# One more of eight weight pairs multiplied in seven block products, with half of its weight sums added by DMA

## The chip, the cores and the metric

The kernel runs on one core of one Trainium2 chip. The metric is the device time of one execution in microseconds (us), as the median of several runs: 1747.23 us before the change (three runs, 1747.02 to 1747.3).

## The reference

One decoder block on 256 tokens with a model width of 2048, all in float32. Cut to what matters here:

```python
u = rmsnorm(h, norm1_g[l])
proj = u @ w_in[l]                       # 2048 x 16896
...                                      # gated recurrence ya, dilated attention yb
mix = sigmoid(gate_a) * ya + sigmoid(gate_b) * yb
h = h + mix @ w_out[l]
v = rmsnorm(h, norm2_g[l])
h = h + conv_ffn(v, w_up[l], conv_w[l], conv_b[l], w_down[l])

def conv_ffn(u, w_up, conv_w, conv_b, w_down):
    hup = u @ w_up                       # 2048 x 11264
    hc = causal_conv(hup, conv_w, width=3) + conv_b
    a, b = hc[..., :5632], hc[..., 5632:]
    return (gelu(a) * b) @ w_down        # 5632 x 2048
```

## The kernel before, in words

**Weights as one stream.** The host lays all weights out in units of 16 tiles of 128x128 (1 MB, `UNIT`), in the order in which they are used. `load(u)` fetches a unit from HBM into one of three buffers `raw` on SP's DMA queue. `split(u)` makes two float32r parts of it: ACT copies with rounding (`hi`), DVE subtracts (`lo = raw - hi`). Every product is then three matmuls: small part of the activations with `hi`, large part with `hi`, large part with `lo`. `begin_unit(u)` splits units up to two ahead of the one in use (`LOOKAHEAD`) and loads a third. The order in which the engines get their instructions is set by the tile framework's scheduler, and each engine works through its own queue in that order; a buffer is reused only after its last reader.

**The up-projection.** `w_up` is computed in 11 blocks of 512 columns of the first half and the 512 matching columns of the second half. In a block there are eight units, one for each pair of 128-row slices of `w_up`; a unit holds a 2x2 matrix of blocks of 128x512, named 11, 21, 12, 22. `UP_PAIRS` says how each pair is multiplied:

- mode P: the eight plain block products, 8 x 3 = 24 matmuls (`PRODUCTS["P"]`). Its unit is split into two halves of 1024 columns.
- mode S: seven block products in the manner of Strassen, 7 x 3 = 21 matmuls (`PRODUCTS["S"]`). They need sums of weight blocks, q1 to q4, which DVE makes in `split_s` out of the loaded unit: four additions of 128x512 (L287, L289, L290, L292), then the splits `sa` (blocks 11 and 21), `se` (22 and q3), `sf` (q2 and q4), each 128x1024, and `sg` (q1), 128x512.

Both modes add into the same seven PSUM banks, `sums[1..7]`. The matching sums of the activations are made once, by `operands`, while the product with `w_out` runs, and kept for all blocks (`hv`). `sevenfold` runs the eight units of a block. `unfold` (L535 to L546) turns the seven sums into the four blocks of the result on ACT and DVE. `hidden_side` then transposes, convolves, gates and splits the result, spread over the following units. From block 2 on, two groups of `w_down` products (`dn`, four units) stand between one block and the next; they write into PSUM banks that `unfold` has read out. Between blocks 0 and 1 and between 1 and 2 no `dn` products stand.

Split halves live in rings of buffers: `hi` and `lo` with four buffers each (`wp`), and for mode S also `se` with four and `sg` and `q` with one.

Of the kernel before, what the change touches and what calls it, by code (L numbers as in the profile page):

```python
# [42 lines left out]
SIDE_US = 1.8  # L43
ALIGN = 136
WARM = 12
# [4 lines left out]
def up_order(b):  # L50

    return (1, 3, 0, 4, 2, 6, 5, 7) if b == 0 else tuple(range(KD // 2))

# [116 lines left out]
def hybrid_block(ctx, tc, x_p, x_t, weights, g1, gf, params, c_rope, c_mask0, c_mask1, c_level, out):  # L170
# [15 lines left out]
    def w4(shape, name, dt=F32):  # L186
        return sb.tile([P] + list(shape), dt, tag="w4", name=name, bufs=21)

    def stage(name):
        return late["stage"].tile([P, 512], F32, tag="o2", name=name, bufs=STAGES)  # L190

    def w1(name, n=T, dt=F32):
        return sbe.tile([P, n], dt, tag="w1", name=name, bufs=10)

# [28 lines left out]

    raws, splits, late = {}, {}, {}
    last = [None, None]
# [16 lines left out]
    def load(u):  # L242
        if u >= NUNITS or u in raws:
            return
        r = wp.tile([P, UNIT * P], F32, tag="raw", name=f"raw{u}", bufs=3)
        n = (4, 2)[u] if u < 2 else 1
        w = UNIT * P // n
        for q in range(n):
            nc.sync.dma_start(r[:, q * w : (q + 1) * w], weights[u, :, q * w : (q + 1) * w])
# [19 lines left out]
    def two_parts(hi, lo, src):  # L269

        act.activation(hi, src, AF.Copy)
        vec.tensor_tensor(lo, src, hi.bitcast(F32), op=ALU.subtract)

    def split_s(u):

        r = raws[u].rearrange("p (b n) -> p b n", b=4)
        pool = late["pool"]

        def pair_tiles(pl, tags, name):
            return [pl.tile([P, 2, 512], F32R, tag=t, name=f"{name}{n}{u}", bufs=b) for n, (t, b) in zip("hl", tags)]  # L280

        q1 = pool.tile([P, 512], F32, tag="q", name=f"q{u}", bufs=1)
        ah, al = pair_tiles(wp, (("hi", 4), ("lo", 4)), "sa")
        eh, el = pair_tiles(pool, (("se", 4), ("se", 4)), "se")
        fh, fl = pair_tiles(pool, (("se", 4), ("se", 4)), "sf")
# [4 lines left out]
        vec.tensor_tensor(r[:, 0], q1, r[:, 2], op=ALU.add)  # L290
# [4 lines left out]
        splits[u] = {  # L295
            "11": (ah[:, 0], al[:, 0]), "21": (ah[:, 1], al[:, 1]), "22": (eh[:, 0], el[:, 0]),
            "q3": (eh[:, 1], el[:, 1]), "q2": (fh[:, 0], fl[:, 0]), "q4": (fh[:, 1], fl[:, 1]), "q1": (g[:, 0], g[:, 1]),
        }

    def split(u):  # L300
# [8 lines left out]
        for s in range(2):  # L309
            hi = wp.tile([P, half], F32R, tag="hi", name=f"hi{u}_{s}", bufs=4)  # L310
            lo = wp.tile([P, half], F32R, tag="lo", name=f"lo{u}_{s}", bufs=4)
            n = 2 if u == 0 else 1
# [163 lines left out]
    def moving(parts, k0, nk, name, pst=None):  # L476
# [218 lines left out]
    def hgrn_side(g, f, k, q, gt, v):  # L695
# [22 lines left out]
        for li, b in enumerate(LEVELS):  # L718
            ps = side_bank(f"lv{g}_{b}")
            psv = ps.rearrange("p (m h t) -> p m h t", m=2, h=HG)  # L720
            ks = sbe.tile([P, M], F32, tag="o2", name=f"ks{g}_{b}", bufs=6)
            act.activation(
# [36 lines left out]
        for m in range(2):  # L759
            po = side_bank(f"ho{g}_{m}")  # L760
            for h in range(HG):
# [3 lines left out]
                pe.matmul(dst, ad[:, m, h], v[:, m, cols], start=(m == 0), stop=True)  # L765
            sq = sbe.tile([P, M], F32, tag="o2", name=f"osq{g}_{m}", bufs=6)
            act.activation(sq, po, AF.Square)
# [5 lines left out]
            vec.reciprocal(sd, sd)  # L773
            o1 = sbe.tile([P, HG, P], F32, tag="o2", name=f"oo{g}_{m}", bufs=6)
            vec.tensor_tensor(
# [159 lines left out]
    def late_bank(i, name):  # L935
        return bank(place[i], name)
# [47 lines left out]
    for b in range(NBLK):  # L984
# [4 lines left out]
        for j, b0, b1 in DOWN.get(b, ()):  # L989
            if b1 == NBLK and not gfb:  # L990
                drain()
                for i in range(2):
                    gfb.append(w4([2, 512], f"gfb{i}"))
                    nc.gpsimd.dma_start(gfb[i].rearrange("p a n -> p (a n)"), gf[:, i * 1024 : (i + 1) * 1024].to_broadcast([P, 1024]))
            pst = moving(ff_parts, b0 * FB, (b1 - b0) * FB, f"dn{b}_{j}", [late_bank(i, f"dn{b}_{j}_{i}") for i in ((4, 3) if j % 2 else (1, 5))])
            for m in range(2):
# [61 lines left out]
```

## Time and profile before

| | before |
|---|---|
| median of 3 runs | 1747.23 us |
| the profiled execution: time, and its span | 1748.37 us, 1746.6 us |
| busy: TensorE (PE) | 1730.5 us, 99% of the span |
| busy: VectorE (DVE) | 1287.3 us, 74% |
| busy: ScalarE (ACT) | 943.0 us, 54% |
| mean granted TensorE clock | 0.996 |
| DMA, mean | 188 GB/s |

The profile is of one execution. Busy times are shares of its span; the remaining 1.8 us of that execution lie outside the span. The up-projection and the `dn` products fill the span from about 1047 us on. In the profile, a matmul of 512 columns is shown with a duration of 0.39 us, but matmuls are pipelined: what one costs is the distance from its start to the next one's start. Queues of an engine's DMA issues are named with a q (SPq).

### The profile page before, as it was taken

Reading aid. Unit: us, or ns where it says so; the run is one execution under the profiler, and the core shown is the slowest. Engines: PE = TensorE matmul, PEld = TensorE weight load, DVE = VectorE, ACT = ScalarE, POOL = GpSimd, SP = SyncE. Lnnn points to the kernel's source line nnn. Section 1 sums busy time; section 2 is a strip of 40 time slices with the busy share of each in tenths; the row PEclk is TensorE's granted clock in tenths of the full one; section 3 lists DMA queues with packets and bytes.
Section 4 is the critical chain, followed back from the end, with each engine's and each line's share of the span. In section 5 each row is a group of like instructions: output and inputs, shape, how many; then the busy total and the mean of one; then the engine's idle time right before and its main releaser. Section 6 shows DMA issues by size and latency. Waiting matters only on the chain.

```text
span 1746.6 us, 21480 instructions
## 1 busy us (share of the span) xinstructions
PE 1730.5 (99%) x8373; PEld 1446.3 (83%) x8373; DVE 1287.3 (74%) x1612; ACT 943.0 (54%) x1166; POOL 9.6 (1%) x25
## 2 busy tenths in 40 slices
PE   9999999999999999999999999999999999999997
PEld 8888888888888888888888888788888888888885
DVE  7765575776858675444656699998988988988975
ACT  6444465555455555444444566665655655655653
POOL 0000000000000000000000000000000000000000
PEclk9999999999999999999999999999999999999998
DMA  7665634444444444556455555445545545546652
GB/s 277 231 204 202 231 141 149 169 169 170 168 169 169 169 168 169 191 194 241 176 188 190 179 207 193 166 175 213 197 165 217 198 164 217 199 162 217 226 183 97
DMA packets 48374, 328.05 MB, mean 188 GB/s; under 512 B 5600, under 2 KB 5856, under 8 KB 10128
## 3 DMA queue, kind: packets, MB, share of 16 engines
q1 hardware_dynamic: 45648, 318.28, 50.7%
q0 software_dynamic: 1472, 5.24, 1.0%
q10 hardware_dynamic: 1152, 3.15, 0.5%
q8 instruction: 66, 1.08, 0.2%
q14 instruction: 36, 0.29, 0.0%
HBM read 321.41 MB, written 2.10 MB: 185 GB/s over the span
## 4 chain that ended last, share of the span: by engine, by line
PE 97%; DVE 2%; DMA 0%; ACT 0%; SPq 0%; issue 0%; DVEq 0%
PE up L527 9%; PE up L525 9%; PE up L526 9%; PE dn L472 5%; PE dn L473 5%; PE dn L474 5%; PE egp L474 3%; PE egp L473 3%; PE egp L472 3%; PE ak L385 3%; PE aq L385 2%; PE wo L474 2%; PE gp L472 2%; PE wo L473 2%; PE gp L473 2%; PE gp L474 2%
## 5 line engine op out<-in xcount | busy, mean ns | idle before, releaser
L319 DVE TENSOR_TENSOR lo<-raw,hi 128x1024 fp32r<-128x1024 f32 (+1 forms) x536 | 651.2, 1218 | 371.7 <-ACT hi L318 363.4
L318 ACT ACTIVATE hi<-raw 128x1024 fp32r<-128x1024 f32 (+1 forms) x536 | 565.7, 1056 | 651.9 <-PE up L526 102.4
L474 PE MATMUL dn<-lo,ff 128*128 128x512 f32 x352 | 138.6, 394 | 0.0
L472 PE MATMUL dn<-hi,ff 128*128 128x512 f32 x352 | 138.3, 395 | 0.0
L473 PE MATMUL dn<-hi,ff 128*128 128x512 f32 x352 | 137.6, 391 | 0.0
L527 PE MATMUL up<-lo,hva 128*128 128x512 f32 x330 | 129.6, 393 | 0.0
L525 PE MATMUL up<-hi,hva 128*128 128x512 f32 x330 | 129.4, 392 | 0.0
L526 PE MATMUL up<-hi,hva 128*128 128x512 f32 x330 | 129.3, 392 | 0.0
L472 PE MATMUL egp<-hi,xu 128*128 128x512 f32 x256 | 100.5, 393 | 0.0
L474 PE MATMUL egp<-lo,xu 128*128 128x512 f32 x256 | 99.8, 390 | 0.0
L473 PE MATMUL egp<-hi,xu 128*128 128x512 f32 x256 | 99.7, 389 | 0.0
L472 PEld LDWEIGHTS dn<-hi,ff 128*128 128x128 f32 x352 | 66.1, 188 | 16.1 <-DVE up5c L544 0.4
L474 PEld LDWEIGHTS dn<-lo,ff 128*128 128x128 f32 x352 | 66.1, 188 | 13.5
L473 PEld LDWEIGHTS dn<-hi,ff 128*128 128x128 f32 x352 | 66.2, 188 | 13.1
L525 PEld LDWEIGHTS up<-hi,hva 128*128 128x128 f32 x330 | 62.1, 188 | 12.6
L527 PEld LDWEIGHTS up<-lo,hva 128*128 128x128 f32 x330 | 62.1, 188 | 12.6
L526 PEld LDWEIGHTS up<-hi,hva 128*128 128x128 f32 x330 | 62.0, 188 | 12.7
L385 PE MATMUL ak<-xu,hi 128*128 128x512 f32 x192 | 68.0, 399 | 0.0
L474 PEld LDWEIGHTS egp<-lo,xu 128*128 128x128 f32 x256 | 48.1, 188 | 9.9
L473 PEld LDWEIGHTS egp<-hi,xu 128*128 128x128 f32 x256 | 48.1, 188 | 9.7
L472 PEld LDWEIGHTS egp<-hi,xu 128*128 128x128 f32 x256 | 48.1, 188 | 9.7
L386 PE MATMUL ak<-xu,lo 128*128 128x256 f32 x192 | 54.0, 281 | 0.0
(548 smaller groups left out, 3876.5 us busy)
## 6 DMA issues: line engine op xcount, KB each, us to landing
raw<-weights SPq DMA_DIRECT2D x298, 1024.0 KB, 4.8
h<-x_t ACTq DMA_DIRECT2D x4, 512.0 KB, 5.9
xt<-x_p SPq DMA_DIRECT2D x3, 512.0 KB, 10.0
xs_q<-aqraw POOLq DMA_DIRECT2D x6, 256.0 KB, 6.8
xs_k<-akraw POOLq DMA_DIRECT2D x6, 256.0 KB, 7.0
raw<-weights SPq DMA_DIRECT2D x4, 256.0 KB, 4.8
raw<-weights SPq DMA_DIRECT2D x2, 512.0 KB, 6.9
gfb<-gf POOLq DMA_DIRECT2D x2, 512.0 KB, 5.3
```

The source lines that it names most:

```text
L318: last[0] = act.activation(hi[:, q * w : (q + 1) * w], raw, AF.Copy)
L319: last[1] = vec.tensor_tensor(lo[:, q * w : (q + 1) * w], raw, hi[:, q * w : (q + 1) * w].bitcast(F32), op=ALU.subtract)
L385: pe.matmul(ps, hi, pair, start=(k == 0), stop=False, skip_group_check=True)
L386: pe.matmul(ps[:, T:], lo, pair[:, :T], start=False, stop=(k == nk - 1), skip_group_check=True)
L472: pe.matmul(pst[m], xl, hi, start=(k == k0), stop=False)
L473: pe.matmul(pst[m], xh, hi, start=False, stop=False)
L474: pe.matmul(pst[m], xh, lo, start=False, stop=(k == k0 + nk - 1))
L525: pe.matmul(sums[b], xl, wh, start=b in fresh, stop=False)
L526: pe.matmul(sums[b], xh, wh, start=False, stop=False)
L527: pe.matmul(sums[b], xh, wl, start=False, stop=left[b] == 0)
```

## The change

- `UP_PAIRS`: four pairs of eight are in mode S instead of three, alternating S and P. `up_order` takes the pairs of a block as P, S, P, S, P, S, P, S (block 0: P, P, S, P, S, P, S, S), where before a block began with S and ended with P.
- `load` of an S unit: block b[3] goes into its place in `raw` and a second time into a buffer `q`; the other three blocks follow in one DMA. Two DMAs issued by GpSimd (POOL) then add on arrival: b[2] onto b[3] (this is q3), b[0] onto `q` (this is q1). DVE keeps two of the four additions (q2 and q4).
- `split` and `split_s` take all buffers out of one ring, `pair`, of [128, 2, 1024] (hi and lo in one): four buffers up to the start of the up-projection and six from then on. `q` gets two buffers.
- The seven products of mode S stand in another order, and the `dn` products with odd j write into the banks of sums 6 and 7 instead of 4 and 3.
- Room: `ALIGN` 136 to 8, `w4` 21 to 22 buffers, `w1` 10 to 8, `o2` 6 to 5 in the recurrence, and `stage` 8 to 6 buffers before the up-projection.

```diff
-UP_PAIRS = "SPSPPSPP"
+UP_PAIRS = "SPSPSPSP"
...
-    return (1, 3, 0, 4, 2, 6, 5, 7) if b == 0 else tuple(range(KD // 2))
+    return (1, 3, 0, 5, 2, 7, 4, 6) if b == 0 else (1, 0, 3, 2, 5, 4, 7, 6)
...
+        if MODES.get(u) == "S":
+            b = [weights[u, :, i * 512 : (i + 1) * 512] for i in range(4)]
+            q1s[u] = late["hv"].tile([P, 512], F32, tag="q", name=f"q{u}", bufs=2)
+            nc.sync.dma_start(r[:, 3 * 512 :], b[3])
+            nc.sync.dma_start(q1s[u], b[3])
+            nc.sync.dma_start(r[:, : 3 * 512], weights[u, :, : 3 * 512])
+            nc.gpsimd.dma_start(r[:, 3 * 512 :], b[2], accum_op=ALU.add)
+            nc.gpsimd.dma_start(q1s[u], b[0], accum_op=ALU.add)
+            raws[u] = r
+            return
...
+    def pair_tile(name):
+        more = late.get("pool")
+        n = ring[0] % (6 if more else 4)
+        ring[0] = (n + 1) if more else (n + 1) % 4
+        pool, bufs = (wp, 4) if n < 4 else (more, 2)
+        return pool.tile([P, 2, 1024], F32R, tag="pair", name=name, bufs=bufs)
...
-        vec.tensor_tensor(q1, r[:, 0], r[:, 3], op=ALU.add)
-        two_parts(ah, al, r[:, 0:2])
-        vec.tensor_tensor(r[:, 3], r[:, 3], r[:, 2], op=ALU.add)
-        vec.tensor_tensor(r[:, 0], q1, r[:, 2], op=ALU.add)
-        two_parts(eh, el, r[:, 2:4])
-        vec.tensor_tensor(r[:, 1], r[:, 1], r[:, 0], op=ALU.add)
-        two_parts(fh, fl, r[:, 0:2])
+        b11, b21 = parts(f"sa{u}", r[:, 0:2])
+        b22, q3 = parts(f"se{u}", r[:, 2:4])
+        vec.tensor_tensor(r[:, 0], q1, r[:, 2], op=ALU.add)
+        vec.tensor_tensor(r[:, 1], r[:, 1], r[:, 0], op=ALU.add)
+        q2, q4 = parts(f"sf{u}", r[:, 0:2])
         g = pool.tile([P, 2, 512], F32R, tag="sg", name=f"sg{u}", bufs=1)
         two_parts(g[:, 0], g[:, 1], q1)
...
-        "S": ((1, "a11", "11"), (7, "x3", "q3"), (6, "x2", "q2"), (2, "a12", "21"), (4, "a22", "q4"), (5, "x1", "q1"), (3, "x4", "22")),
+        "S": ((1, "a11", "11"), (2, "a12", "21"), (7, "x3", "q3"), (3, "x4", "22"), (6, "x2", "q2"), (4, "a22", "q4"), (5, "x1", "q1")),
...
-            pst = moving(..., [late_bank(i, ...) for i in ((4, 3) if j % 2 else (1, 5))])
+            pst = moving(..., [late_bank(i, ...) for i in ((6, 7) if j % 2 else (1, 5))])
```

How the loads of a block now stand in the queues. On SP before, in block 5, one DMA for each unit (`raw` numbers are the buffers' running numbers; 10210, 10318 and 10468 are units in mode S, the others P):

```order
L249 DMA raw_10210<-weights 128x2048
L249 DMA raw_10273<-weights 128x2048
L249 DMA raw_10318<-weights 128x2048
L249 DMA raw_10385<-weights 128x2048
L249 DMA raw_10427<-weights 128x2048
L249 DMA raw_10468<-weights 128x2048
```

On SP now, in block 7 (S units: `raw` 10906, 11015, 11107, 11181, with their `q` numbered one higher):

```order
L253 DMA raw_10906<-weights 128x512
L255 DMA raw_10906<-weights 128x1536
L261 DMA raw_10962<-weights 128x2048
L253 DMA raw_11015<-weights 128x512
L255 DMA raw_11015<-weights 128x1536
L254 DMA q_11108<-weights 128x512
L261 DMA raw_11071<-weights 128x2048
L253 DMA raw_11107<-weights 128x512
L255 DMA raw_11107<-weights 128x1536
L254 DMA q_11182<-weights 128x512
L261 DMA raw_11152<-weights 128x2048
```

And on POOL now, the adding DMAs of the same units; before, POOL had nothing to do in this part of the program:

```order
L257 DMA q_10907<-weights 128x512
L257 DMA q_11016<-weights 128x512
L256 DMA raw_10906<-weights 128x512
L256 DMA raw_11015<-weights 128x512
L257 DMA q_11108<-weights 128x512
L256 DMA raw_11107<-weights 128x512
L257 DMA q_11182<-weights 128x512
L256 DMA raw_11181<-weights 128x512
```

An S unit now takes three DMAs on SP and two on POOL instead of one on SP; the `q` ones go ahead of their unit, since `q` has a buffer free earlier.

On PE, the end of a block's up-projection and the start of `dn`. Before (block 2), the last product of a block is one of mode P, into sum 3, and the last one into sum 5 stands two products earlier:

```order
L527 MATMUL up_5_8763<-lo_1_9006,hva_8022 128x512
L525 MATMUL up_3_8761<-hi_1_9005,hvd_8023 128x512
L526 MATMUL up_3_8761<-hi_1_9005,hvd_8023 128x512
L527 MATMUL up_3_8761<-lo_1_9006,hvd_8023 128x512
L525 MATMUL up_3_8761<-hi_1_9005,hvd_8023 128x512
L526 MATMUL up_3_8761<-hi_1_9005,hvd_8023 128x512
L527 MATMUL up_3_8761<-lo_1_9006,hvd_8023 128x512
L472 MATMUL dn_0_1_9124<-hi_0_9039,ff_0_8635 128x512
```

Now (block 6), the last product is one of mode S, into sum 5:

```order
L539 MATMUL up_4_10495<-sf_10710,hvs_7673 128x512
L540 MATMUL up_4_10495<-sf_10710,hvs_7673 128x512
L541 MATMUL up_4_10495<-sf_10710,hvs_7673 128x512
L539 MATMUL up_5_10496<-sg_10713,hvx_7674 128x512
L540 MATMUL up_5_10496<-sg_10713,hvx_7674 128x512
L541 MATMUL up_5_10496<-sg_10713,hvx_7674 128x512
L486 MATMUL dn_0_1_10817<-hl_0_10739,ff_0_10054 128x512
```

The `dn` products follow at once; the first 24 of them write into bank 1, and only then comes the one (`dn_0_5`) that reuses the bank of sum 5.

On PE, the boundary between blocks 1 and 2, where no `dn` stands. Before, the next block opens with products of mode S into sums 1, 7, 6 and 1 (11 matmuls, the last five of them here), and then needs the bank of sum 2:

```order
L525 MATMUL up_6_8764<-sfh_8667,hvx_7475 128x512
L526 MATMUL up_6_8764<-sfh_8667,hvx_7475 128x512
L527 MATMUL up_6_8764<-sfl_8668,hvx_7475 128x512
L525 MATMUL up_1_8759<-sah_8767,hvs_7652 128x512
L526 MATMUL up_1_8759<-sah_8767,hvs_7652 128x512
L525 MATMUL up_2_8760<-sah_8663,hvs_7474 128x512
L526 MATMUL up_2_8760<-sah_8663,hvs_7474 128x512
```

Now it opens with two matmuls into sum 1 and goes on with sum 2; the first into sum 5 is the thirteenth matmul (the two into sum 1 ahead of these rows counted, the transpose L963 not):

```order
L539 MATMUL up_2_8417<-hl_0_8325,hva_7174 128x512
L540 MATMUL up_2_8417<-hl_0_8325,hva_7174 128x512
L541 MATMUL up_2_8417<-hl_0_8325,hva_7174 128x512
L539 MATMUL up_2_8417<-hl_0_8325,hva_7174 128x512
L540 MATMUL up_2_8417<-hl_0_8325,hva_7174 128x512
L541 MATMUL up_2_8417<-hl_0_8325,hva_7174 128x512
L963 MATMUL ua1t_8478<-ident,up1c_8403 128x128
L541 MATMUL up_1_8416<-sa_8362,hvs_7158 128x512
L539 MATMUL up_2_8417<-sa_8362,hvs_7158 128x512
L540 MATMUL up_2_8417<-sa_8362,hvs_7158 128x512
L541 MATMUL up_2_8417<-sa_8362,hvs_7158 128x512
L539 MATMUL up_5_8420<-hl_1_8328,hva_7174 128x512
```

The banks of sums 2 and 5 are both written again sooner than before: that of sum 2 after two matmuls instead of 11, that of sum 5 after 12 instead of 17.

More of the change, by code (lines that the diff above doesn't have):

```diff
@@ L186, in w4 @@
     def w4(shape, name, dt=F32):
-        return sb.tile([P] + list(shape), dt, tag="w4", name=name, bufs=21)
+        return sb.tile([P] + list(shape), dt, tag="w4", name=name, bufs=22)
     def stage(name):
-        return late["stage"].tile([P, 512], F32, tag="o2", name=name, bufs=STAGES)
+        return late["stage"].tile([P, 512], F32, tag="o2", name=name, bufs=STAGES if "pool" in late else STAGES - 2)
     def w1(name, n=T, dt=F32):
-        return sbe.tile([P, n], dt, tag="w1", name=name, bufs=10)
+        return sbe.tile([P, n], dt, tag="w1", name=name, bufs=8)
     def small(shape, name, tag, bufs=2):
@@ L222, in pc @@
         return par[:, POFF[name][0] + i : POFF[name][0] + i + 1]
-    raws, splits, late = {}, {}, {}
+    raws, splits, late, q1s = {}, {}, {}, {}
+    ring = [0]
     last = [None, None]
@@ L290, in split_s, with parts @@
-        vec.tensor_tensor(r[:, 0], q1, r[:, 2], op=ALU.add)
-        two_parts(eh, el, r[:, 2:4])
-        vec.tensor_tensor(r[:, 1], r[:, 1], r[:, 0], op=ALU.add)
-        two_parts(fh, fl, r[:, 0:2])
+        pool, q1 = late["pool"], q1s[u]
+        def parts(name, src):
+            t = pair_tile(name)
+            hi, lo = t[:, 0].rearrange("p (b n) -> p b n", b=2), t[:, 1].rearrange("p (b n) -> p b n", b=2)
+            two_parts(hi, lo, src)
+            return [(hi[:, i], lo[:, i]) for i in range(2)]
@@ L309, in split @@
         for s in range(2):
[L310 to L311 removed]
+            t = pair_tile(f"hl{u}_{s}")
+            hi, lo = t[:, 0], t[:, 1]
             n = 2 if u == 0 else 1
```

22 lines of the change are left out of this document (6 added, 16 removed).

## The prediction

> **What bounds the kernel now.** I read the page first, then the waits and the windows of five whole blocks of the up-projection, then single rows. From the page: the span, the busy times, DVE's busy tenths in 40 slices of the span, and the shares by engine of the chain that ended last.
>
> ```profile
> span 1746.6 us, 21480 instructions
> PE 1730.5 (99%) x8373; PEld 1446.3 (83%) x8373; DVE 1287.3 (74%) x1612; ACT 943.0 (54%) x1166; POOL 9.6 (1%) x25
> ...
> DVE  7765575776858675444656699998988988988975
> ...
> PE 97%; DVE 2%; DMA 0%; ACT 0%; SPq 0%; issue 0%; DVEq 0%
> ```
>
> The windows' header, one block and the sum of the five:
>
> ```profile
> core 0: us, PE busy (x) PEld busy (x) DVE busy (x) ACT busy (x) POOL busy (x), PEclk, DMA share, GB/s
> 1275.64:1341.04 65.40, 65.40 (x296) 53.80 (x295) 56.43 (x73) 38.23 (x46) 0.00 (x0) 1.00 0.55 194
> sum 327.04, PE 327.04 PEld 268.96 DVE 282.16 ACT 190.89 POOL 0.00; mean PE 65.41 PEld 53.79 DVE 56.43 ACT 38.18 POOL 0.00
> ```
>
> PE is the chain, 97% of it, and in a block of 65.40 us it is never idle (65.40 busy). DVE has 9 us free in a block, ACT 27 us, the DMA engines about half of theirs. Who waits in those five blocks (engine and line, for whom, us in total, times, longest):
>
> ```profile
> ACT hi L318 <- PE up L526: 53.7, 43, 2.5
> ACT hi L318 <- DMA raw<-weights: 3.5, 5, 0.9
> SPq L249 <- DVE lo L319: 192.9, 45, 7.1
> ```
>
> The splitting waits for PE to free a buffer, seldom for a load; the loads wait for the splitting to free a `raw` buffer. So the feeders run ahead of PE until the rings are full, and what PE no longer has to do is saved as long as this stays so. What one matmul costs is the distance of starts; the timeline has them, and the load of the S unit whose first product (`sah`) is the fourth row of PE:
>
> ```profile
> 1289.11 0.33 SPq L249 DMA_DIRECT2D raw<-weights  x1
> ...
> 1308.24 0.39 PE L525 MATMUL up<-hi,hvd 128*128 128x512 f32 x1
> 1308.47 0.39 PE L526 MATMUL up<-hi,hvd 128*128 128x512 f32 x1
> 1308.69 0.39 PE L527 MATMUL up<-lo,hvd 128*128 128x512 f32 x1
> 1308.92 0.39 PE L525 MATMUL up<-sah,hvs 128*128 128x512 f32 x1
> 1309.15 0.39 PE L526 MATMUL up<-sah,hvs 128*128 128x512 f32 x1
> ```
>
> Four steps take 0.91 us, 0.2275 us each. Counted in program order, the load issued at 1289.11 is this S unit's: 19.8 us ahead of its use.
>
> **The fourth pair in mode S.** A block had 3 x 21 + 5 x 24 = 183 matmuls and gets 4 x 21 + 4 x 24 = 180. Three fewer in each of 11 blocks are 33 x 0.2275 = 7.5 us, all on the path: a block shrinks from 65.40 to 64.72 us. This is the whole gain; the other parts can only eat it.
>
> **DVE and ACT.** Rows of one block (busy us, mean ns):
>
> ```profile
> L319 DVE TENSOR_TENSOR lo<-raw,hi 128x1024 fp32r<-128x1024 f32 x18 | 22.0, 1220 | 8.5 <-ACT hi L318 8.5
> L272 DVE TENSOR_TENSOR sel<-raw,seh 128x1024 fp32r<-128x1024 f32 x3 | 3.7, 1217 | 0.0
> L272 DVE TENSOR_TENSOR sg<-q,sg 128x512 fp32r<-128x512 f32 x3 | 2.0, 683 | 0.0
> L290 DVE TENSOR_TENSOR raw<-q,raw 128x512 f32<-128x512 f32 x3 | 2.0, 681 | 0.0
> L318 ACT ACTIVATE hi<-raw 128x1024 fp32r<-128x1024 f32 x19 | 20.2, 1061 | 22.6 <-PE up L526 11.0 <-PE dn L473 6.9 <-issue 2.5
> L271 ACT ACTIVATE seh<-raw 128x1024 fp32r<-128x1024 f32 x3 | 3.2, 1052 | 0.0
> L271 ACT ACTIVATE sg<-q 128x512 fp32r<-128x512 f32 x3 | 1.9, 622 | 0.0
> ```
>
> DVE: an S unit's subtractions are 3 x 1.217 + 0.683 = 4.33 us, a P unit's 2 x 1.220 = 2.44, so +1.89; additions fall from 12 to 8, -4 x 0.681 = -2.72. DVE goes from 56.43 to 55.6 us of a block of 64.7, 86% as before. ACT: 3 x 1.052 + 0.622 - 2 x 1.061 = +1.66, to 39.9 us, 62%. Neither is on the path, so neither the relief nor the load changes the sum; the cover is the 9 and 25 us that they have free.
>
> **The loads.** An S unit brings 256 (block 3) + 256 (its copy) + 768 + 2 x 256 (the adds) = 1792 KB instead of 1024. Rows for landing (KB each, median us from issue to landing; the last two rows are windows, one of the block's dense part, one from the start of the program):
>
> ```profile
> raw<-weights SPq DMA_DIRECT2D x298, 1024.0 KB, 4.8
> xs_k<-akraw POOLq DMA_DIRECT2D x6, 256.0 KB, 7.0
> gfb<-gf POOLq DMA_DIRECT2D x2, 512.0 KB, 5.3
> lev<-c_level POOLq DMA_DIRECT2D x1, 448.0 KB, 9.2
> 1298.00:1340.00 42.00, 42.00 (x189) 34.73 (x189) 35.16 (x45) 24.37 (x30) 0.00 (x0) 1.00 0.58 210
> 10.00:30.00 20.00, 19.48 (x98) 15.94 (x97) 16.83 (x19) 16.10 (x22) 0.00 (x0) 1.00 0.90 365
> ```
>
> *Bandwidth.* A block has 12 units of 1024 KB; at 0.55 of 65.4 us one costs 3.0 us of all 16 engines. Now they are 12 + 4 x 0.75 = 15, 45 us of 64.7 (0.70). Where S and P alternate, 2.75 units are 8.2 us in the 45 x 0.2275 = 10.2 us that PE takes for a pair of units (0.81); if an add costs twice its bytes, since it also reads its target, 3.25 units are 9.8 us (0.95). The start of the program ran at 0.90. So the load is dense but fits, at the upper end only just.
>
> *Latency.* No row shows an adding DMA. From below it is a POOL DMA of the same stage (`gfb`, 5.3 us); from above the slowest one (`lev`, 9.2) or twice the common 7.0, if the bytes move twice: 14. I take 7.0, the row with the same size. Block 3 lands in 4.8 (the full unit's time), the add 7.0 later, `se` is split in 1.05 + 1.22: 14.1 us after the issue. PE needs it with the third product, 19.8 + 6 x 0.2275 = 21.2 us after the issue. That leaves 7 us.
>
> *Throughput of the three `raw` buffers.* A P unit holds one for at least 4.8 + 2 x 1.06 + 1.22 = 8.1 us, an S unit for 4.8 + 7.0 + 2 x (1.05 + 1.22) + 2 x 0.68 = 17.7. In three pairs of units (30.7 us of PE) each buffer serves one P and one S, 25.8 us. Margin 4.9 us: an add may take up to 11.9 us before the ring, and not PE, sets the pace. By the row I chose it costs nothing.
>
> *Queues.* SP issues 20 DMAs a block instead of 12, at 0.33 us each 2.6 us more, on a queue that mostly waits. A `q` load stands ahead of the next P load and waits for DVE's `sg`; that split comes with the unit whose `raw` buffer the P load waits for anyway, so it delays little. On POOL each add waits for its plain load, and the adds behind it wait too; the plain loads were issued on SP in a compatible order, so no add waits for a load issued after its own. POOL is otherwise idle here.
>
> A rule speaks against the adds. The `gfb` row above is a POOL DMA in this stage, with DVE 87% busy (52.26 of 60 us):
>
> ```profile
> 1590.00:1650.00 60.00, 60.00 (x273) 49.31 (x273) 52.26 (x69) 34.20 (x42) 1.09 (x2) 1.00 0.58 210
> ```
>
> It landed in 5.3 us, so a busy DVE did not hold it. The Trainium skill ("SBUF — State Buffer", section "SBUF: two separate sides") warns that a DMA issued from POOL waits for its descriptors while DVE runs an operation that uses both ports; by that rule each add would land later, and the late-add rival below would be nearer. It names single-source fp32 copies, which the rows above do not contain, so I give it no part of the sum.
>
> **The order of units and products; the rings.** With `dn` between blocks, 24 matmuls (5.5 us) cover the later end of sum 5, and PE does not wait. Between blocks 0 and 1 and between 1 and 2 there is no such cover. The timeline shows the price of that before, and the windows the clock after it:
>
> ```profile
> 1101.39 0.50 PE L525 MATMUL up<-sah,hvs 128*128 128x512 f32 x1 [2.12 <-DVE up1c L542]
> 1098.00:1101.30 3.30, 1.28 (x6) 0.74 (x4) 3.30 (x5) 0.20 (x1) 0.00 (x0) 1.00 0.78 308
> 1101.30:1106.00 4.70, 4.61 (x14) 3.62 (x15) 4.70 (x8) 1.70 (x2) 0.00 (x0) 0.64 0.66 232
> ```
>
> PE waited 2.1 us for `unfold`, and then ran 4.7 us at a clock of 0.64, another 0.36 x 4.7 = 1.7 us: 3.8 us in all. `unfold` was late because DVE was: it has the side work of the last block to do and no `dn` time to do it in, and was busy without a break:
>
> ```profile
> 1090.00:1098.00 8.00, 8.00 (x37) 6.59 (x37) 8.00 (x12) 6.40 (x9) 0.00 (x0) 1.00 0.12 49
> ```
>
> After the change DVE has 0.8 us less to do in such a block and PE 0.7 us less, so DVE is as late as before. From below this is -3.8 (the wait goes). From above, the next block now needs the bank of sum 2 after two matmuls instead of 11 and that of sum 5 after 12 instead of 17, and DVE, which works in order, has the `se` of an S unit ahead of `unfold`. That unit's load goes out when the third unit before it is split; from then on DVE has some 9.4 us of splitting until this `se` (3 x 0.68 + 6 x 1.22), the add lands after 11.8, so DVE stands still for 2.4 us. With a clock drop of 1.7 that is 4.1 us at each of two boundaries, +8.2. I take 0, the row itself: the wait stays. The Trainium skill ("TensorE: Matmul & The Clock Gate", section "Part 1: The HAM clock gate") puts the idle time that halves the clock at about 3.4 us; here 2.1 us of idleness was followed by a low clock, so the measurement decides, and a new wait of 2 us costs nearly double.
>
> The larger `pair` ring takes nothing from PE. Fewer buffers (`w1`, `o2`, `stage`) touch the part before 1047 us, the first 24 slices, where DVE is busy 4 to 8 tenths and PE's order hardly changes: 0, within 1 us either way. The fourth S operand costs some subtractions of 128 columns on DVE, once: 0 under the product with `w_out`.
>
> **Sum.** -7.5. On the profiled execution, 1748.37 - 7.5 = 1740.9; it stood 1.1 us above the median, so the median comes to 1739.7 us.
>
> **Rivals.**
> 1. *The wait at the block boundary vanishes.* For it: `unfold`'s reading of sum 2 now stands right behind that of sum 6 on DVE, ahead of a split. Against: DVE as busy as before. 1739.7 - 3.8 = 1735.9.
> 2. *The boundaries between blocks 0 and 2 eat the gain.* For it: DVE without a break there, the adds ahead of `unfold`, two S units in a row at the end of block 0. Against: before, only one of the two boundaries waited. 1739.7 + 8.2 = 1747.9 at most, half of it 1743.8.
> 3. *The adds land late (slower).* If an add takes 14 us, a buffer's P and S last 32.8 us instead of 25.8, the pace of a pair is 10.9 instead of 10.2 us, and 44 pairs lose 0.7 each: +31, 1770. It decides from 11.9 us for an add on; a pace of 0.17 us more for a pair (7.5 / 44) already eats the gain, which is 12.4 us. For it: nothing shows an add, and the DMA engines are at 0.81 to 0.95. Against: all POOL rows land in 9.2 us or less, and the units of `dn` let the ring catch up.
> That the change does less than it says can be left out: the 33 matmuls are gone from PE's queue.
>
> **Chances.** Forecast 0.50, rival 1 0.15, rival 2 0.17, rival 3 0.18. A difference of 0.2% (3.5 us) is about what a measurement can tell here, so faster (below 1743.7) is 0.65, same 0.17, slower 0.18. The range reaches from 1735.0 (rival 1) to 1750.0, past rival 2 and a ring that is a little too slow; rival 3 at its price lies outside. The forecast alone has 1738 to 1743.
>
> **What would show it.** Right: 33 matmuls fewer; windows of a block at 64.7 us with PE never idle; DVE near 55.6, ACT near 39.9, DMA share near 0.70; POOL adds landing in 6 to 9 us. Wrong: `se` on ACT waiting for DMA in every block, PE waiting for `se` or `sf`, a PE clock below 1.00 inside the blocks, or PE waiting for `unfold` longer than 2 us between blocks 0 and 2.

## The result: 4.2% slower

| kernel | median, us | against before |
|---|---|---|
| before | 1747.26 (4 runs, 1747.02 to 1747.81) | |
| after | 1821.28 (4 runs, 1819.32 to 1824.3) | 1.0418, 95% interval 1.0405 to 1.0431 |

The profiled execution of after took 1824.3 us, its span is 1822.5. The page of after, with span, busy times, the clock in 40 slices, the shares of the chain that ended last, and the two groups of `se` (busy, mean ns, idle time ahead and what ended it):

```profile
span 1822.5 us, 21674 instructions
PE 1749.0 (96%) x8340; PEld 1451.6 (80%) x8340; DVE 1286.4 (71%) x1592; ACT 954.7 (52%) x1188; POOL 86.4 (5%) x113
...
PEclk9999999999999999999999988999999999999998
...
PE 78%; DMA 10%; DVE 7%; ACT 3%; issue 2%; SPq 0%; ACTq 0%; POOLq 0%; DVEq 0%
...
L284 DVE TENSOR_TENSOR se<-raw,se 128x1024 fp32r<-128x1024 f32 x44 | 53.6, 1217 | 61.0 <-ACT se L283 60.8
L283 ACT ACTIVATE se<-raw 128x1024 fp32r<-128x1024 f32 x44 | 46.6, 1058 | 83.7 <-DMA raw<-weights 71.3
```

The 33 matmuls are gone (8373 to 8340), and PE is no longer the whole chain: DMA has 10% of it. `se` on ACT waited 71.3 us for DMA, which is the q3 add. Of seven whole blocks, taken from the first `dn` product of one to that of the next, one window and the sum:

```profile
1308.28:1381.40 73.12, 66.70 (x292) 54.14 (x293) 56.44 (x71) 39.12 (x48) 6.98 (x8) 0.97 0.73 218
sum 505.74, PE 469.83 PEld 381.75 DVE 395.15 ACT 273.81 POOL 49.15; mean PE 67.12 PEld 54.54 DVE 56.45 ACT 39.12 POOL 7.02
```

A block takes 505.74 / 7 = 72.2 us and not 65.4. The timeline shows where in a block; the rows are those of the end of block 5 (columns: start, duration, engine, line, in brackets the idle time ahead and what ended it):

```profile
1351.07 0.33 SPq L253 DMA_DIRECT2D raw<-weights  x1
1357.10 0.33 SPq L261 DMA_DIRECT2D raw<-weights  x1
1357.63 0.88 POOL L256 DMA_DIRECT2D raw<-weights  x1 [6.61 <-DVE sf L284]
1359.37 0.33 SPq L261 DMA_DIRECT2D raw<-weights  x1
1359.92 0.87 POOL L257 DMA_DIRECT2D q<-weights  x1 [1.42 <-DMA q<-weights]
1368.23 1.06 ACT L283 ACTIVATE se<-raw 128x1024 fp32r<-128x1024 f32 x1 [7.45 <-DMA raw<-weights]
1373.61 0.33 SPq L261 DMA_DIRECT2D raw<-weights  x1
1375.13 0.39 PE L541 MATMUL up<-sg,hvx 128*128 128x512 f32 x1
1379.71 1.06 ACT L332 ACTIVATE hl<-raw 128x1024 fp32r<-128x1024 f32 x1 [2.60 <-DMA raw<-weights]
1380.68 0.67 ACT L552 ACTIVATE up5c<-up,rstd_r 128x512 f32<-128x512 f32 x1
1381.40 0.79 PE L486 MATMUL dn<-hl,ff 128*128 128x512 f32 x1 [5.88 <-ACT up5c L552]
1381.99 0.63 PE L487 MATMUL dn<-hl,ff 128*128 128x512 f32 x1
1382.42 0.63 PE L488 MATMUL dn<-hl,ff 128*128 128x512 f32 x1
```

This is the last S unit of the block. Its block 3 is issued at 1351.07 and its q3 add at 1357.63. Loads of 1 MB for `dn` units go out on both sides of the add, at 1357.10 and at 1359.37, and at 1359.92, 2.3 us after it, the `q` add of the next block's first S unit. ACT gets q3 at 1368.23, after 7.45 us of waiting with everything behind it, so a `raw` buffer comes free late (the unit's last split, `sf`, ends on DVE at 1373.58), the next load on SP goes out only at 1373.61, and ACT waits another 2.60 us for that one. Behind that split stands `unfold`'s last read of sum 1 (L552), and the first `dn` product wants that bank. PE stands still for 6 us and then steps 0.43 us instead of 0.2275.

How long the q3 adds took from issue to landing (the arrival of the data), over these blocks, and what the DMA engines did during the one above (queues: q1 is SP's, q0 is POOL's; packets, MB, share of the 16 engines' time):

```profile
DMA to landing us min/median/max: 4.0/4.5/10.9
```

```profile
q1 hardware_dynamic: 454, 2.40, 62.4%
q0 software_dynamic: 274, 0.51, 31.9%
```

Three adds of a block land in 4 to 5 us; the fourth takes 9.3 to 10.9. In the window above the engines are 94% busy, a third of it with 0.51 MB of adds. Which of its neighbours makes that add late, the second add or the loads of 1 MB, these rows do not tell; some of the experiments below bear on it. The same view of one whole block, of before (1275.64 to 1341.04) and of after (1308.28 to 1381.40), gives the price of an add:

```profile
q1 hardware_dynamic: 1736, 12.65, 54.6%
```

```profile
q1 hardware_dynamic: 2962, 13.79, 53.0%
q0 software_dynamic: 1152, 2.10, 19.5%
```

A plain load costs 0.546 x 65.4 x 16 / 12.65 = 45 us of one engine for a MB, an add 0.195 x 73.12 x 16 / 2.10 = 109, 2.4 times as much.

**Where the time went.** Three stretches of each kernel, cut in the timeline at PE's first `up` product, the first `dn` product (blocks 0 to 2 lie before it) and the first `dn` product of the last block, in us:

| | blocks 0 to 2 | a block, mean of 8 | rest | median |
|---|---|---|---|---|
| before | 133.8 | 65.39 | 79.4 | 1747.3 |
| after | 153.9 | 72.10 | 80.9 | 1821.3 |
| all sums on DVE | 144.8 | 64.73 | 79.3 | 1754.8 |
| last unit's q3 on DVE | 157.0 | 64.67 | 79.5 | 1766.5 |
| q1 by DMA, q3 on DVE | 146.4 | 66.85 | 79.5 | 1771.6 |
| q3 by DMA, q1 on DVE | 153.5 | 65.12 | 80.9 | 1768.8 |
| copies, no adds | 147.6 | 67.69 | 79.2 | 1784.2 |
| other bank | 160.0 | 70.67 | 89.9 | 1825.1 |
| one `q` buffer | 172.3 | 76.56 | 81.9 | 1876.5 |
| all on DVE, old order | 142.5 | 64.64 | 79.1 | 1749.7 |
| the same, 3 S pairs in blocks 0, 1 | 133.3 | 64.70 | 79.1 | 1741.8 |
| all on DVE, old order, POOL's additions in blocks 0, 1 | 147.5 | 64.57 | 79.1 | 1756.6 |

After lost 20.1 us in blocks 0 to 2 and 8 x 6.71 = 53.7 in the blocks behind them; with 1.5 at the end and 0.7 ahead that is the 75.9 us between the spans.

### The profile page after: what moved, and what is told of

Read it like the earlier page. It is cut to its first block, busy times and chain, and to the rows that moved or that the text cites. A ratio compares the mean times of both kernels' runs of the same rounds, so it can differ in the third digit from the quotient of the medians.

```text
span 1822.5 us, 21674 instructions
## 1 busy us (share of the span) xinstructions
PE 1749.0 (96%) x8340; PEld 1451.6 (80%) x8340; DVE 1286.4 (71%) x1592; ACT 954.7 (52%) x1188; POOL 86.4 (5%) x113
## 4 chain that ended last, share of the span: by engine, by line
PE 78%; DMA 10%; DVE 7%; ACT 3%; issue 2%; SPq 0%; ACTq 0%; POOLq 0%; DVEq 0%
DMA raw<-weights 10%; PE dn L486 5%; PE dn L487 5%; PE dn L488 5%; PE egp L486 3%; PE egp L488 3%; PE egp L487 3%; PE up L539 3%; PE up L541 3%; PE up L540 3%; PE ak L399 2%; DVE hl L333 2%; PE aq L399 2%; PE wo L486 2%; PE gp L486 2%
## 5 line engine op out<-in xcount | busy, mean ns | idle before, releaser
L333 DVE TENSOR_TENSOR hl<-raw,hl 128x1024 fp32r<-128x1024 f32 (+1 forms) x514 | 621.4, 1218 | 326.3 <-ACT hl L332 325.2
L332 ACT ACTIVATE hl<-raw 128x1024 fp32r<-128x1024 f32 (+1 forms) x514 | 539.3, 1054 | 574.8 <-PE egp L488 79.1
L486 PE MATMUL dn<-hl,ff 128*128 128x512 f32 x352 | 146.1, 417 | 38.9 <-ACT up5c L552 5.9
L487 PE MATMUL dn<-hl,ff 128*128 128x512 f32 x352 | 144.2, 410 | 0.0
L488 PE MATMUL dn<-hl,ff 128*128 128x512 f32 x352 | 143.6, 408 | 0.0
L486 PEld LDWEIGHTS dn<-hl,ff 128*128 128x128 f32 x352 | 69.9, 198 | 57.8 <-ACT up5c L552 6.3
L539 PE MATMUL up<-hl,hva 128*128 128x512 f32 x264 | 104.1, 395 | 5.3 <-DVE up1c L556 3.2
L541 PE MATMUL up<-hl,hva 128*128 128x512 f32 x264 | 104.5, 396 | 0.0
L540 PE MATMUL up<-hl,hva 128*128 128x512 f32 x264 | 104.2, 395 | 0.0
L486 PE MATMUL egp<-hl,xu 128*128 128x512 f32 x256 | 100.5, 393 | 0.0
L488 PE MATMUL egp<-hl,xu 128*128 128x512 f32 x256 | 99.8, 390 | 0.0
L487 PE MATMUL egp<-hl,xu 128*128 128x512 f32 x256 | 99.7, 389 | 0.0
L284 DVE TENSOR_TENSOR se<-raw,se 128x1024 fp32r<-128x1024 f32 x44 | 53.6, 1217 | 61.0 <-ACT se L283 60.8
L283 ACT ACTIVATE se<-raw 128x1024 fp32r<-128x1024 f32 x44 | 46.6, 1058 | 83.7 <-DMA raw<-weights 71.3
L488 PEld LDWEIGHTS dn<-hl,ff 128*128 128x128 f32 x352 | 69.7, 198 | 14.9
L487 PEld LDWEIGHTS dn<-hl,ff 128*128 128x128 f32 x352 | 70.0, 199 | 13.9
L284 DVE TENSOR_TENSOR sa<-raw,sa 128x1024 fp32r<-128x1024 f32 x44 | 53.8, 1222 | 24.9 <-ACT sa L283 24.8
L399 PE MATMUL ak<-xu,hl 128*128 128x512 f32 x192 | 68.0, 399 | 0.0
L539 PEld LDWEIGHTS up<-hl,hva 128*128 128x128 f32 x264 | 50.3, 190 | 17.2 <-DVE up1c L556 3.9
```

Source lines behind the costliest of these rows:

```text
L332: last[0] = act.activation(hi[:, q * w : (q + 1) * w], raw, AF.Copy)
L333: last[1] = vec.tensor_tensor(lo[:, q * w : (q + 1) * w], raw, hi[:, q * w : (q + 1) * w].bitcast(F32), op=ALU.subtract)
L399: pe.matmul(ps, hi, pair, start=(k == 0), stop=False, skip_group_check=True)
L486: pe.matmul(pst[m], xl, hi, start=(k == k0), stop=False)
L487: pe.matmul(pst[m], xh, hi, start=False, stop=False)
L488: pe.matmul(pst[m], xh, lo, start=False, stop=(k == k0 + nk - 1))
```

## The experiments

**All four sums on DVE.** In the changed kernel:

```diff
-            nc.sync.dma_start(r[:, 3 * 512 :], b[3])
-            nc.sync.dma_start(q1s[u], b[3])
-            nc.sync.dma_start(r[:, : 3 * 512], weights[u, :, : 3 * 512])
-            nc.gpsimd.dma_start(r[:, 3 * 512 :], b[2], accum_op=ALU.add)
-            nc.gpsimd.dma_start(q1s[u], b[0], accum_op=ALU.add)
+            nc.sync.dma_start(r, weights[u])
...
+        vec.tensor_tensor(q1, r[:, 0], r[:, 3], op=ALU.add)
...
+        vec.tensor_tensor(r[:, 3], r[:, 3], r[:, 2], op=ALU.add)
```

> The changed kernel, but a unit in mode S is loaded whole by one DMA on SP and all four weight sums are made by DVE; order of units, products, ring and banks stay as changed. Late-add theory (the last S unit's add of a block lands 9.4 to 10.9 us after its issue, ACT's se waits for it, a raw buffer comes free late, a dn load goes out late, and ACT reads bank 1 out late, 5 to 6 us of PE and a low clock behind it per block): the stalls are gone and the time falls from 1821 to 1738 to 1755; DVE rises by 8 x 0.68 = 5.4 us to some 61 of 64.7 us of a block, and what is left of the loss would be DVE's. Rival one (the new order of products, the one ring of six, the smaller buffers or the banks of dn cost the time): it stays above 1800. Rival two (DVE, now 94% busy in a block, becomes the pace): 1760 to 1790, with PE waiting for splits on DVE inside the blocks.

1754.8 us, 1.0042 (1.0027 to 1.0057), at the upper end of what the late-add theory had. 66 of the 74 us belong to the adds and the loads that feed them: with them gone a block is 64.73 us, although DVE has eight additions more. What is left lies in blocks 0 to 2. PE's waits between 1040 and 1165 us there (for whom, total, times, longest):

```profile
PE up L537 <- ACT up1c L550: 4.2, 1, 4.2
PE up L537 <- ACT up0c L550: 2.3, 1, 2.3
PE up L537 <- DVE up0c L554: 1.8, 1, 1.8
PE up L537 <- DVE up1c L554: 1.6, 1, 1.6
PE dn L484 <- ACT up2c L550: 1.6, 1, 1.6
```

All are waits for `unfold`, at both boundaries without `dn` and at the first with it.

**The last S unit's q3 on DVE.** The unit is loaded whole and DVE adds q3; q1, and q3 of the other three, stay with DMA:

```diff
+            late_add = LAST_S.get(u, False)
+            if late_add:
+                nc.sync.dma_start(q1s[u], b[3])
+                nc.sync.dma_start(r, weights[u])
...
+        if LAST_S.get(u, False):
+            vec.tensor_tensor(r[:, 3], r[:, 3], r[:, 2], op=ALU.add)
```

> The changed kernel, but the last of the four S units of each block is loaded whole and its q3 is made by DVE; the other three keep the adding DMA, and all four keep q1 by DMA. Late-add theory: only the last unit's add is late (9.4 to 10.9 us against 4.0 to 5.0), so one addition of 0.68 us on DVE in each block takes away the stall between up and dn: 1745 to 1765, at most the stalls of the first two boundaries (some 20 us in the changed kernel) are left. Rival (the adds of all units hold up the ring together, so that the lateness moves on to the third unit or into the block): above 1790.

1766.5 us, 1.0109 (1.0092 to 1.0126), just past the range. One addition in a block gave back 55 us, and a block with the other seven adds takes 64.67:

```profile
1232.00:1296.70 64.70, 64.70 (x294) 53.21 (x293) 57.17 (x73) 39.46 (x49) 6.11 (x7) 1.00 0.76 243
```

PE is busy throughout, with the DMA engines at 0.76. So the adds do not hold up the blocks as such; the q3 add at the end does, with the way its unit is loaded. In blocks 0 to 2 this kernel is the slower one (157.0 against 153.9), and no run here says why.

**q1 by DMA, q3 on DVE.**

```diff
-            nc.sync.dma_start(r[:, 3 * 512 :], b[3])
             nc.sync.dma_start(q1s[u], b[3])
-            nc.sync.dma_start(r[:, : 3 * 512], weights[u, :, : 3 * 512])
-            nc.gpsimd.dma_start(r[:, 3 * 512 :], b[2], accum_op=ALU.add)
+            nc.sync.dma_start(r, weights[u])
...
+        vec.tensor_tensor(r[:, 3], r[:, 3], r[:, 2], op=ALU.add)
```

> The changed kernel, but only q1 is made by DMA (copy and adding DMA into the q buffer, wanted last of all in a unit); a unit in mode S is loaded whole and q3 is made by DVE, so three additions on DVE, 58.3 us of 64.7. Late-add theory: nothing that frees a raw buffer waits for an add any more, so the stalls are gone: 1738 to 1752, and less DVE work than with all four sums on DVE (5 to 10 us better than that kernel if DVE sets the pace there, equal if it doesn't). Rival (any adding DMA beside the loads slows them): above 1780.

1771.6 us, 1.0139 (1.0117 to 1.0161): a miss for the late-add theory, which had 1738 to 1752, and for its rival, which had more than 1780; it is slower than with all sums on DVE. No `raw` buffer waits for an add here, but adds and loads slow each other. First the loads of 1 MB (median landing), then the `q` adds (landing), both from about 1157 to 1692 us:

```profile
raw<-weights SPq DMA_DIRECT2D x96, 1024.0 KB, 6.0
```

```profile
DMA to landing us min/median/max: 4.1/7.1/9.2
```

In the same stretch of before, and of the kernel with all sums on DVE, the median of these loads is 4.8 us. How much of the 1.2 us is due to the adds and how much to the plain loads into `q` was not tried apart. The slowest add, with the loads issued around it:

```profile
1463.42 0.33 SPq L259 DMA_DIRECT2D raw<-weights  x1
1464.62 0.88 POOL L255 DMA_DIRECT2D q<-weights  x1 [16.52 <-DVE hl L332]
1465.69 0.33 SPq L254 DMA_DIRECT2D raw<-weights  x1
```

No other add is under way, and it takes 9.2 us, with one load of 1 MB issued 1.2 us ahead of it and one 1.1 us behind. In eight places of this stretch the loads stand so, and there an add takes 8.2 to 9.2 us.

**q3 by DMA, q1 on DVE.**

```diff
-            nc.gpsimd.dma_start(q1s[u], b[0], accum_op=ALU.add)
...
+        vec.tensor_tensor(q1, q1, r[:, 0], op=ALU.add)
```

> The changed kernel, but the q buffer is only loaded (block 3, plain DMA) and DVE adds block 0 to it, so POOL issues only the four adds that make q3; three additions on DVE, 58.3 us of 64.7. If the last S unit's add lands late because the add for q1 of the next block travels beside it (issued 2.3 us behind it), it now lands in 4 to 6 us as for the other units and the stall at dn goes: 1755 to 1770. If it is late because two plain loads of 1 MB are issued around it, it stays at 9 to 11 us and the time at 1805 to 1822.

1768.8 us, 1.0121 (1.0105 to 1.0137), in the range of the first case. The q3 adds over the same blocks:

```profile
DMA to landing us min/median/max: 3.9/4.2/5.0
```

The 10.9 is gone, and a block takes 65.12. But this does not show that the second add was the cause, since the loads of 1 MB have moved too. The end of block 5 in this run:

```profile
1340.73 0.88 POOL L256 DMA_DIRECT2D raw<-weights  x1 [12.28 <-DVE sg L283]
1343.86 0.33 SPq L260 DMA_DIRECT2D raw<-weights  x1
1346.14 0.33 SPq L260 DMA_DIRECT2D raw<-weights  x1
```

They go out 3.1 and 5.4 us behind the add, the second after it has landed; in the changed kernel it was 0.5 us ahead and 1.7 behind. The last block of both kernels speaks for the loads. No `q` add follows there, only two plain loads of 512 KB by POOL (`gfb`), 0.5 and 1.1 us behind the q3 add in both. In the changed kernel loads of 1 MB go out 0.7 us ahead of the add and 1.6 behind, and it lands in 10.6 us; here the first one goes out 3.1 us behind, and it lands in 4.4. The loss in blocks 0 to 2 stays (153.5).

**Copies in place of adds.**

```diff
-            nc.gpsimd.dma_start(r[:, 3 * 512 :], b[2], accum_op=ALU.add)
-            nc.gpsimd.dma_start(q1s[u], b[0], accum_op=ALU.add)
+            nc.gpsimd.dma_start(r[:, 3 * 512 :], b[2])
+            nc.gpsimd.dma_start(q1s[u], b[0])
```

> The changed kernel with the same DMAs in the same queues and order, but the two that POOL issues for a unit copy and do not add (the weight sums q3 and q1 are left out of the computation: q3 becomes block 2 and q1 becomes block 0). If an add is slow because it reads its target before it writes, the copies land in 3 to 4 us, the last one of a block in 5 to 7, and the time is 1755 to 1775. If it is POOL's queue beside the dense loads that is slow, whatever it carries, the last copy of a block still lands in 9 to 11 us and the time is 1810 to 1822.

1784.2 us, 1.0215 (1.0189 to 1.0241), between the two theories. POOL's queue in a block (1292.7 to 1360.3), and the landing of the copies that stand for q3:

```profile
q0 software_dynamic: 640, 2.10, 11.6%
```

```profile
DMA to landing us min/median/max: 3.3/3.6/7.6
```

A copied MB costs 0.116 x 67.6 x 16 / 2.10 = 60 us of an engine, so of an add's 109 some 49 go with the adding. Part of these 49 may be the price of smaller packets, which was not tried apart: the copies bring the 2.10 MB in 640 packets, the adds in 1152. The last copy of a block lands in 6.2 to 7.6 us, where the last add took 9.3 to 10.9. Half of the loss (37 of 74 us) goes with the adding; the other half is left when POOL's DMAs only copy.

**One `q` buffer.**

```diff
-            q1s[u] = late["hv"].tile([P, 512], F32, tag="q", name=f"q{u}", bufs=2)
+            q1s[u] = late["hv"].tile([P, 512], F32, tag="q", name=f"q{u}", bufs=1)
```

> The changed kernel with one q buffer instead of two, all adding DMAs kept: a unit's q is loaded and added to only after the S unit before it is split, so the add for the next block's q1 can't travel beside the last add for q3 of a block any more. If it is the two adds beside each other that make the last one take 10.5 us, it now lands in 4 to 7 us, the stall of some 5 us before dn shrinks to 0 to 2 in the eight blocks, and the time is 1765 to 1785 (the stalls of blocks 0 to 2 stay). If the bytes of the adds as such, or the plain loads beside them, make it late, it stays at 9 to 11 us and the time at 1810 to 1825; the same if q, loaded later, becomes late itself, but then DVE's addition that makes q2 waits for the DMA into q, and not ACT's se.

1876.5 us, 1.0729 (1.0711 to 1.0747). The last clause of the expectation came true, though the time is 51 us past the range that it had. The last q3 add of a block landed in 4.0 us (first row, block 5; 3.9 to 4.5 in the eight blocks), but `q` became late instead (waits between 1164 and 1800 us):

```profile
DMA to landing us min/median/max: 4.0/4.0/4.0
```

```profile
DVE raw L307 <- DMA q<-weights: 86.6, 17, 7.4
```

This is no cure, and it does not part the two neighbours of the late add either: the `q` add goes out 5.2 us behind the q3 add here (1389.18 after 1384.01), but the loads of 1 MB, too, only 3.1 and 5.3 us behind it. No run has the loads of 1 MB around the last q3 add and nothing else on POOL's queue, or the second add without the loads. What there is (8.2 to 9.2 us for a lone `q` add between two such loads, 10.6 us in the last block without a second add) points to the loads; how much the second add puts on top stays open.

**Another bank for the first `dn` products.**

```diff
-            pst = moving(..., [late_bank(i, ...) for i in ((6, 7) if j % 2 else (1, 5))])
+            pst = moving(..., [late_bank(i, ...) for i in ((6, 7) if j % 2 else (8, 5))])
```

> The changed kernel, but the dn products with even j write into the bank of sum 8, which nothing of the block uses late, and that of sum 5, instead of 1 and 5. The loads and adds stay as late as they are. If PE stands at the first dn because bank 1 is read out late by ACT (behind the splits of a late dn unit), the 24 products into the other bank cover it: the 5 to 6 us and the low clock behind them go in each of 8 or 9 blocks, about 45 to 55 us, and 1765 to 1780 is left. Rival (PE stands for the split weights of the dn unit or for the bank of sum 5): the stall only moves by a few products and the time stays at 1810 to 1822.

1825.1 us, 1.0443 (1.0427 to 1.0459): no gain, as the rival had it, though 3 us past its range. The 24 products run, and then PE waits for the bank of sum 5:

```profile
1313.43 0.39 PE L486 MATMUL dn<-hl,ff 128*128 128x512 f32 x1
1317.72 0.79 PE L486 MATMUL dn<-hl,ff 128*128 128x512 f32 x1 [3.89 <-DVE up4c L558]
```

DVE's read of sum 5 (L558) stands behind the same late split as ACT's of sum 1. The bank that the wait names was only the last link of the chain. A block is 1.4 us shorter, and the last stretch (9.0 longer than in the changed kernel) and blocks 0 to 2 (6.1) take that back.

**The old order, all sums on DVE.** On top of the first experiment:

```diff
-    return (1, 3, 0, 5, 2, 7, 4, 6) if b == 0 else (1, 0, 3, 2, 5, 4, 7, 6)
+    return (1, 3, 0, 2, 5, 4, 6, 7) if b == 0 else tuple(range(KD // 2))
...
-((1, "a11", "11"), (2, "a12", "21"), (7, "x3", "q3"), (3, "x4", "22"), ...
+((1, "a11", "11"), (7, "x3", "q3"), (6, "x2", "q2"), (2, "a12", "21"), ...
```

> All four weight sums on DVE and units loaded whole, as in the first experiment (1754.8), and besides the order of before: pairs of a block as S, P, S, P, S, P, S, P (block 0: P, P, S, S, P, P, S, P), the products of mode S as before, odd dn products into the banks of sums 4 and 3. The ring of six pair tiles stays. If the new order is what cost at the boundaries between blocks 0, 1 and 2 (12.6 us of stalls there in the first experiment, 2.3 before), about 8 to 12 us come back: 1742 to 1747, at or just under the kernel before. If DVE's load does it (eight additions more in a block than the changed kernel has), the stalls stay whatever the order, and it stays at 1752 to 1757.

1749.7 us, 1.0013 (1.0004 to 1.0023), between the two: 5 us came back by the medians, and of the 11.0 us that the first experiment had lost against before in blocks 0 to 2, 8.7 are still there (142.5 against 133.8). Around the stall that remains, the window and PE's rows:

```profile
1098.00:1112.00 14.00, 7.76 (x20) 4.85 (x19) 13.96 (x18) 5.98 (x9) 0.00 (x0) 0.63 0.42 150
```

```profile
1102.37 0.79 PE L537 MATMUL up<-sa,hvs 128*128 128x512 f32 x1 [3.19 <-ACT up1c L550]
1106.08 0.79 PE L537 MATMUL up<-sf,hvx 128*128 128x512 f32 x1 [2.06 <-DVE up1v L548]
```

DVE is busy 13.96 of 14 us. That led to the next.

**Three S pairs in blocks 0 and 1.** On top of the old order:

```diff
+def up_pairs(b):
+    return "SPSPSPPP" if b < 2 else UP_PAIRS
...
-    return (1, 3, 0, 2, 5, 4, 6, 7) if b == 0 else tuple(range(KD // 2))
+    return (1, 3, 0, 5, 2, 6, 4, 7) if b == 0 else (0, 1, 2, 3, 6, 4, 5, 7) if b == 1 else tuple(range(KD // 2))
...
```

> The kernel with the old order and all sums on DVE (1749.7), but blocks 0 and 1 have three pairs in mode S as before (order P, P, S, P, S, P, S, P and S, P, S, P, P, S, P, P); blocks 2 to 10 keep four. The pair that changes its mode has the operands of both modes (4 KB taken from the w4 ring, 21 buffers as before). If the stalls at the boundaries come from DVE being full in blocks without dn (13.96 of the 14 us around the stall, 56.45 of the 58 us ahead of it), DVE has 4.6 us less to do in each of the two blocks and the stalls fall back to the 2.3 us of the kernel before: 1747.4 less 9 x 3 x 0.2275 = 6.1 us, so 1739 to 1744. If the lead is lost because of the ring of six tiles or the fourth pair in the later blocks, it stays at 1747 to 1750.

1741.8 us (6 runs, 1739.79 to 1743.91), 0.9972 (0.996 to 0.9984): as expected, and 0.3% faster than before. Four blocks' sum of windows (1207.07 to 1465.94):

```profile
sum 258.87, PE 258.63 PEld 212.93 DVE 243.71 ACT 157.97 POOL 0.00; mean PE 64.66 PEld 53.23 DVE 60.93 ACT 39.49 POOL 0.00
```

DVE at 60.9 of 64.7 us is enough where `dn` stands between the blocks. Of the gain on the kernel ahead, 9.2 us lie in blocks 0 to 2 of the profiled executions. Another 1.9 lie ahead of them, where `w4` has one buffer fewer. The order of the units in blocks 0 and 1 changes along with their number of S pairs; none of this was tried apart.

**POOL's own additions.** On the old order with four S pairs, q1 and q3 of blocks 0 and 1 are added by POOL's instructions:

```diff
+        adds = nc.gpsimd if u in FIRST_S else vec
...
-        vec.tensor_tensor(q1, r[:, 0], r[:, 3], op=ALU.add)
+        adds.tensor_tensor(q1, r[:, 0], r[:, 3], op=ALU.add)
...
```

> The kernel with the old order and all sums on DVE (1749.7), but in blocks 0 and 1 POOL adds q1 and q3 by its own instructions instead of DVE (16 additions of 128x512). If DVE's time alone decides there, it has 16 x 0.68 = 10.9 us less to do, as much as the stalls and the low clock behind them, and the time falls to 1742 to 1746. If an addition takes POOL over 3 us or slows DVE's instructions beside it, ACT's splits wait for POOL and nothing is gained: 1748 to 1756.

1756.6 us, 1.0056 (1.0043 to 1.007): the second case, 0.6 us past its range. The groups of POOL, and of DVE between 1040 and 1110 us (busy, mean ns):

```profile
L303 POOL TENSOR_TENSOR q<-raw 128x512 f32<-128x512 f32 x8 | 20.2, 2531 | 859.5 <-DMA raw<-weights 854.8 <-DVE raw L308 4.7
L305 POOL TENSOR_TENSOR raw<-raw 128x512 f32<-128x512 f32 x8 | 14.5, 1809 | 0.6
```

```profile
L333 DVE TENSOR_TENSOR hl<-raw,hl 128x1024 fp32r<-128x1024 f32 x11 | 16.0, 1477 | 0.0
```

An addition that takes DVE 0.68 us takes POOL 1.8 to 2.5 on the mean, and DVE's subtractions go from a mean of 1.22 to one of 1.48 us: most stay at 1.21, and single ones beside POOL's additions take up to 2.3. The Trainium skill ("SBUF — State Buffer", section "Who interferes with whom") says that a DVE instruction with two inputs in SBUF contends with a GpSimd instruction that reads SBUF; this run agrees.

## Why the prediction was wrong, step by step

**"The fourth pair in mode S": right.** Where nothing else stalls PE, a block takes 64.6 to 64.7 us (five kernels of the table), against 64.72 foretold.

**"DVE and ACT": right in what it said of the path.** 56.45 and 39.12 us of a block, against 55.6 and 39.9; behind block 2 neither set the pace.

**"Bandwidth": mis-sized.** It took an add's bytes as a load's, or twice that at most; they cost 2.4 times. A block's DMA comes to (13.79 x 45 + 2.10 x 109) / 16 = 53 us of all engines, 0.82 of 64.7 and not 0.70. And the mean over a pair hid the place: at a block's end the next block's `q` add, the q3 add and the loads of 1 MB meet.

**"Latency": mis-sized, and not the wait that counted.** It took 7.0 us for every add. Three adds of a block land in 4.0 to 5.0 us, faster than its lower bound, and the last in 9.3 to 10.9, inside its bounds, and every block has one: a single value hid that. (The row that it took was a busy one: its transfers go in pairs 0.5 us apart, at 79.21 and 79.71 us for one, with a load of 1 MB beside them.) The last unit's block 3 took 5.9 us too, and the add went out 6.6 us after it. From the first issue to the end of the `se` split that is 19.5 us, not 14.1. Even so PE did not wait for `se`: it came to that product at 1371.03, 0.5 us after the split had ended. Of the 7 us that the step left, 0.5 was left; the time was lost elsewhere.

**"Throughput of three raw buffers": right as an average, and the wrong question.** No q3 add reached 11.9 us. But the engines work in order: one late `se` held ACT for 7.45 us, with the `dn` splits and `unfold` behind it, however well the ring did on average.

**"With dn between blocks … PE does not wait": the step that failed.** It waited 4.5 to 5.9 us in each of eight blocks. The step looked at when sum 5 is wanted, and had no term for what stands ahead of `unfold` in ACT's and DVE's queues: the split of a `dn` unit whose load waits for the buffer of the unit with the late add. With the slow steps behind the stall that is the 7.4 us that a block lost, and one addition of a block given back to DVE took away 55 us of the 74.

**"The order of units and products": its zero was wrong, its upper bound near.** Without any add, blocks 0 to 2 took 11.0 us more than before, against the bound of 8.2. The runs agree with the cause that it named, DVE without a break, but do not show it alone: the old order gives 2 to 5 us back, and three S pairs instead of four in blocks 0 and 1, with another order of units there and one `w4` buffer fewer, the rest. The step counted 0.8 us less for DVE because the adds were to be DMA's; the adds themselves then cost another 9 us in these blocks (153.9 against 144.8), and those for q3 alone nearly as much (153.5).

**"Queues": the delay was on the engines behind it.** POOL and SP issued in time (POOL's add 0.6 us after block 3 had landed). The rule that it gave no part, of DVE holding POOL's descriptors, did not show in the issues: those of the adds took 0.86 to 0.89 us, all of them. The `q` load sent ahead, which it took as harmless, lets the next block's `q` add go out beside the last q3 add; whether that costs much is not settled. The Trainium skill ("DMA: Bandwidth & Descriptors", section "Queues, rings and completion order") says that a DMA engine goes round between its queues packet by packet. The window of the late add has 274 packets of q0 and 454 of q1 and does not show their order, so no run here tests that; that the queues slow each other is measured (6.0 against 4.8 us for a load of 1 MB).

Rival 3 had the sign and the cause, an add that lands late, but priced it through the ring, 0.7 us for each of 44 pairs and 1770. The way that the time went is one stall and its slow clock for each of eight blocks, and the boundaries of blocks 0 to 2.

## What to carry to other kernels

One value for a transfer, taken from a row or a median, says nothing of the place where it is slowest. Price it again at the busiest place of the program, with the transfers that are issued just ahead of it and behind it. A late operand costs more than its own wait when the engine that waits works in order: look at what stands behind it and who needs that. And where a stage lacks the cover that the others have (here `dn`), size the work for it separately: four S pairs paid only in the blocks that had it.

## What the runs showed of the hardware

- A MB that POOL's queue adds in SBUF took 109 us of one DMA engine, copied by the same queue 60, loaded in 1 MB units by SP's 45.
- An add of 256 KB (q3) landed in 4 to 5 us in the middle of a block; one (`q`) between two loads of 1 MB, issued some 1 us ahead of it and behind it, in 8.2 to 9.2; one (q3) between two such loads, with a second add or other loads by POOL behind it, in 9.3 to 10.9.
- The median landing of a load of 1 MB was 6.0 us with `q` adds and loads into `q` in the blocks, 4.8 without.
- POOL took 1.8 to 2.5 us on the mean for an addition of 128x512 that takes DVE 0.68, and DVE's subtractions took a fifth longer on the mean.
